# A two-layer decoder trunk: the fill of a head pair in the order keys, V, queries, little of it in the pair's last step, and more of the memory attentions' fill in their drain

## The chip, the cores and the metric

The kernel runs on one core of a Trainium2 chip. The metric is the device time of one execution in microseconds (us), lower is better. The engines are TensorE (PE; PEld is its weight load, which runs beside the matmuls), VectorE (DVE), ScalarE (ACT), GpSimd (POOL), and the queue of SyncE (SP), which issues the DMAs.

## The reference, cut to what matters

The input x is 1024 tokens by 1024 features, the memory 256 tokens. There are two layers, each x <- LayerNorm(alpha x + y W_out). In both, one part of y is a 4-head cross-attention into the memory, gated by silu. The other part is a pooling branch in layer 0 and, in layer 1, a causal attention of 16 heads of 64 with forget gates, whose keys and values come from one shared projection:

```python
def forgetting_attention(u, k, v, cum):
    ...
        logits = jnp.einsum('bqhd,bkhd->bhqk', qi, k,
                            preferred_element_type=jnp.float32) * scale
        logits = logits + (ci[..., :, None] - cum_k[:, :, None, :])
    ...
        logits = jnp.where(mask[None, None], logits, -jnp.inf)
        p = jax.nn.softmax(logits, axis=-1)
        return jnp.einsum('bhqk,bkhd->bqhd', p.astype(v.dtype), v)

def mixer_sublayer(x, mem, w_in, w_mem_kv, w_out, main_fn):
    h = x @ w_in
    ...
    y = jnp.concatenate([y_main * jax.nn.silu(g_main), y_mem * jax.nn.silu(g_mem)], axis=-1)
    return y @ w_out
```

All is float32.

## The kernel before, in words

**Products.** A float32 operand is kept as a high and a low part in a rounded float32 format, and a product is three matmuls (high·high, high·low, low·high). The unit of a projection is `slab` (L171 to L188): 128 output features by 1024 tokens, 48 matmuls of 128x512 with float32 accumulation in two PSUM banks of the three named `pj`. The weights come in two pieces, each loaded by SP into `raw` (three buffers) and split into high and low (`split_w`, L145 to L154; in the attention stage by POOL). The order is piece 0 for the token halves n = 0 and 1, 12 matmuls each, then piece 1 for n = 0 and 1. When a bank is complete its `evac` function is issued: after matmul 36 for the first 512 tokens, after matmul 48 for the others. `slab` is a generator: it yields after each matmul, so other code can be put between.

**Stages, in time.** Pool group 0 and the memory's keys and values for layer 0 (to about 110 us), memory attention 0 (to about 195), pool groups 1 to 3 (to about 340), the output projection with LayerNorm of layer 0 (to about 480), the memory's keys and values and memory attention 1 (about 535 to 625), the start units (first V, forget gates, the first pair's keys and queries, to about 684), the forgetting attention `fox` (684 to 1136), and the output projection of layer 1 (to the end).

**What sets the order.** PE's order is the order of the code, written out by hand within `manual_schedule` (L312, L771). The order on DVE, ACT, POOL and SP is set by the tile scheduler. `Fill` (L42 to L63) is a list of such generators; `pump(cols)` issues matmuls until `cols` columns (512 each) are due, so projections are spread as fill over the steps of an attention.

**`mem_attention`** (L259 to L325). After the memory queries, four gates' slabs (4 x 48 matmuls) are the fill of a loop of ten steps t. In steps 0 to 7 `probs(t)` makes the softmax of four heads for 128 tokens: logits on PE, maximum on DVE, Exp on ACT, the normalised probabilities in two half-precision parts on ACT and DVE (the latter is L294), and a transposing DMA. In the odd steps from 3 on, `values` makes O for 256 tokens and four heads; one PSUM bank `O` is read each time by DVE (L310). Steps 8 and 9 are the drain. Five calls of `pump` in each step issue a `part` of what is left (L314, L317, L321).

**`fox`** (L717 to L769). Sixteen heads, two to a pair, so eight pairs; eight steps to a head, from tile 7 (128 queries by 1024 keys) down to tile 0 (128 by 128). After head 15 come five steps without logits. A step is:
- `probs` (L631 to L657): POOL applies the causal mask to the row of forget gates (L640); PE makes the logits into a bank `L` (L169); DVE adds the gates and takes the extreme value (L647); ACT makes Exp into a bank `T` (L653).
- between logits and Exp, `halves` of the tile before (L659 to L672): DVE normalises (L664 to L667), ACT (L670) and DVE (L671) write two half-precision parts.
- 40% of the step's fill (`FRAC`), then `turn` (L676): a transposing DMA on SP's queue.
- for an even tile of five steps ago (`LAG`), `values` (L682 to L697): O on PE, read by ACT (L696) and DVE (L697); in the odd head also `pair_out` on POOL.
- 60% of the fill.

The fill of a pair p > 0 is what pair p + 1 needs, from `pair_units` (L604 to L610): the keys' slab (`k_evac`, L583 to L589, with two swaps of halves by DMA), the queries' slab, and V's slab for p + 1 >= 2. The queries' `q_evac` (L594 to L599) has for each half of 512 tokens and for each head of the pair one ACT copy (L596) and one DVE subtraction (L597), 64x512 each. V's bank is copied by ACT (L609) to `u`; `values_of` (L490) takes the maximum (L236), scales and splits it (L237 to L244) and turns it by two DMAs (L500). The V of pairs 0 and 1 was made in the start units (`first_vs`). Pairs 0, 2, 4 and 7 have gates' slabs added behind; pair 0's fill is the remainder of pair 1's units after the start units; pair 7 has the late gates.

What is left of the fill is divided over the steps left of the pair by `SHARE` (L39), all ones; pair 7's also over the five steps of the drain (L742, L743). At the end of an odd head the rest is issued (L768, L769). A pair's 144 matmuls are thus 9 in each of its 16 steps (12 in pairs 2 and 4).

Of the kernel before, what the change touches and what calls it, by code (L numbers as in the profile page):

```python
# [35 lines left out]
LAG = 5  # L36
APART = 6 * NH
PSCALE = 2.0 ** 15
SHARE = (1,1,1,1,1,1,1,1)  # L39


class Fill:  # L42
# [29 lines left out]
def trunk_kernel(ctx, tc, x, xT, memT, win, wk, wv0, wv, wmk, wmv, wout, poolw, pscale, lng, lnb, bforget, out):  # L72
# [186 lines left out]
    def mem_attention(l, XH, XL, kv, qtile, ytile, yd):  # L259

        kh, kl, v, undo = kv
        qs = []
        for h in range(MH):
            qh, ql = qtile(), qtile()
            run(slab(win[l, 8 + h], XH, XL, lambda cols, acc: hi_lo(qh[:, cols], ql[:, cols], acc)))
            qs.append((qh, ql))
        ys, gs = [ytile() for _ in range(MH)], [G() for _ in range(MH)]
        pt, fill = {}, Fill()
        for h in range(MH):
            fill.add(gate_units(win[l, 20 + h], gs[h], XH, XL), SLAB)  # L270

        def probs(i):

            p, two = sb([P, MH, NMEM], "P", 4), sb([P, 2, MH, NMEM], "P", 4, F16)
            m, ms, sm, r = tiny(MH), tiny(MH), tiny(MH), tiny(MH)
            for hp in range(2):
                lg = ps([P, 2, NMEM], "L", 2)
                for j in range(2):
                    h = 2 * hp + j
                    qh, ql = (t[:, i * P : (i + 1) * P] for t in qs[h])  # L280
                    mm3(lg[:, j, :], ((qh, kh[:, h, :]), (qh, kl[:, h, :]), (ql, kh[:, h, :])))
                pair = slice(2 * hp, 2 * hp + 2)
                nc.vector.tensor_reduce(m[:, pair], lg, AX.X, ALU.max, negate=True)
                nc.vector.tensor_scalar(ms[:, pair], m[:, pair], MSCALE, None, ALU.mult)
                for j in range(2):
                    h = 2 * hp + j
                    nc.scalar.activation(
                        p[:, h, :], lg[:, j, :], AF.Exp, bias=ms[:, h : h + 1], scale=MSCALE, accum_out=sm[:, h : h + 1],
                    )
            nc.vector.tensor_scalar(r, sm, 1.0 / PSCALE, None, ALU.mult)  # L290
            nc.vector.reciprocal(r, r)
            for h in range(MH):
                nc.scalar.activation(two[:, 0, h, :], p[:, h, :], AF.Copy, scale=r[:, h : h + 1])
                nc.vector.scalar_tensor_tensor(  # L294
                    two[:, 1, h, :], p[:, h, :], r[:, h : h + 1], two[:, 0, h, :], ALU.mult, ALU.subtract,
                )
            pt[i] = T([P, 2, MH, 2, P], F16)
            nc.sync.dma_start_transpose(
                pt[i].rearrange("p e h m q -> p (e h m) q"), two.rearrange("p e h t -> p (e h t)"),
            )  # L300

        def values(c, h):
            acc = ps([P, 2 * P], "O", 1)
            for j in range(2):
                t = pt[2 * c + j]
                mm3(acc[:, j * P : (j + 1) * P], [
                    (v[:, h, 2 * e + m, :], t[:, f, h, m, :])
                    for m in range(2) for e, f in ((0, 0), (0, 1), (1, 0))
                ])
            nc.vector.tensor_scalar(ys[h][:, c * 2 * P : (c + 1) * 2 * P], acc, undo[:, h : h + 1], None, ALU.mult)  # L310

        with tc.manual_schedule(engines={PE}):  # L312
            for t in range(ST + 2):
                part = fill.left / (5 * (ST + 2 - t))  # L314
                if t < ST:
                    probs(t)
                fill.pump(part if t <= ST else 3 * part)  # L317
                for h in range(MH):
                    if t >= 3 and t % 2 == 1:
                        values((t - 3) // 2, h)  # L320
                    fill.pump(part if t <= ST else part / 2)  # L321
            fill.pump(float("inf"))
        for h in range(MH):
            nc.vector.tensor_tensor(ys[h], ys[h], gs[h], ALU.mult)  # L324
            nc.sync.dma_start(yd[:, h, :], ys[h])  # L325
# [150 lines left out]
    with tc.tile_pool(name="in1", bufs=1) as in1:  # L476

        def xy():
            return sb([P, S], "B", 10, F32R, in1)
# [98 lines left out]
        def qk_units(p):  # L578

            halves = (slice(0, 64), slice(64, P)), (slice(64, P), slice(0, 64))  # L580
            ks, ws = ([xy() for _ in range(2)] for _ in range(2))

            def k_evac(cols, acc):  # L583
                for t, w, (own, other) in zip(ks, ws, halves):
                    nc.scalar.copy(t[own, cols], acc[own, :])
                    nc.vector.tensor_tensor(t[other, cols], acc[own, :], t[own, cols].bitcast(F32), ALU.subtract)
                    if cols.stop == S:
                        for to, of in ((own, other), (other, own)):
                            nc.sync.dma_start(w[to, :].bitcast(F32), t[of, :].bitcast(F32))  # L589

            yield from slab(wk[p], XH, XL, k_evac)
            qs = [xy() for _ in range(2)]

            def q_evac(cols, acc):  # L594
                for t, (own, other) in zip(qs, halves):
                    nc.scalar.activation(t[own, cols], acc[own, :], AF.Copy, scale=-0.125)  # L596
                    nc.vector.scalar_tensor_tensor(  # L597
                        t[other, cols], acc[own, :], -0.125, t[own, cols].bitcast(F32), ALU.mult, ALU.subtract,
                    )  # L599

            yield from slab(win[1, p], XH, XL, q_evac)
            pairs[p] = list(zip(qs, ks, ws))

        def pair_units(p):  # L604

            yield from qk_units(p)
            if p >= 2:
                u = MK([P, S], F32)
                yield from slab(wv[p - 2], XH, XL, lambda cols, acc: nc.scalar.copy(u[:, cols], acc))  # L609
            pairs[p].append(first_vs[p] if p < 2 else values_of(u))  # L610

        def start_units(own, following):

# [103 lines left out]
        def fox(following):  # L717
# [8 lines left out]
            for hd in range(HEADS + 1):  # L726
                pr, b = divmod(hd, 2)
                if hd < HEADS:
                    if b == 0:
                        o, sums = G(), sb([P, 4 * ST], "sums", 2, F32, small).rearrange("p (n b i) -> p n b i", n=2, b=2)  # L730
                        if 0 < pr < 7:
                            fill.add(pair_units(pr + 1), 3 * SLAB)
                        for ahead in {0: (0, 1), 2: (2,), 4: (4,), 7: (7,)}.get(pr, ()):
                            gate_ahead(ahead)
                        if pr == 0:
                            fill.add(following, SLAB)
                        for late in (3, 5, 6) if pr == 7 else ():
                            fill.add(late_gate(late), SLAB)
                    R, ahead_R = ahead_R, None
                for i in range(ST if hd < HEADS else LAG):  # L740
                    tile_of = ST - 1 - i
                    ahead = sum(SHARE[i:]) + (sum(SHARE) if b == 0 else 0) + (sum(SHARE[:LAG]) if pr == 7 else 0)  # L742
                    part = fill.left * SHARE[i] / (ahead if hd < HEADS else sum(SHARE[i:LAG]))  # L743
                    new, split = None, []

                    def behind():
                        if fresh[0]:
                            split.append(halves(*fresh[0]))
                            fresh[0] = None

                    if i == 2 and hd < HEADS - 1:
                        ahead_R = forget_rows(hd + 1)
                    if hd < HEADS:
                        new = (hd, tile_of, o)
                        fresh[0] = probs(hd, tile_of, R, sums, behind)
                    else:
                        behind()
                    fill.pump(part * FRAC[0])
                    for what in split:
                        turn(*what)  # L760
                    older = past[0]
                    if older and older[1] % 2 == 0:
                        values(older[0], older[1] // 2, older[2])
                        if older[0] % 2:
                            pair_out(older[0] // 2, older[1] // 2, older[2], gs.get(older[0] // 2))
                    fill.pump(part * (1 - FRAC[0]))
                    past = past[1:] + [new]
                if b and pr < 7 or hd == HEADS:  # L768
                    fill.pump(float("inf"))  # L769
# [71 lines left out]
```

## Time and profile before

| | |
|---|---|
| runs | 1290.47, 1286.43, 1284.64 us |
| median | 1286.43 us |
| the profiled execution | 1286.64 us |
| its span in the trace | 1284.6 us |
| mean granted TensorE clock | 0.993 |
| busy share of the span | PE 97%, PEld 81%, DVE 62%, ACT 45%, POOL 13% |
| matmuls with their line | 2928 of L181 (the slabs) 724.7 us; 384 logits 91.8 us; 1152 of O in `fox` 76.2 us |

A row of a timeline is: start, duration, engine, line, operation, output tile <- input tiles, shapes, count, and in brackets the idle time before it with what ended it. A row like `PE L L169 <- DVE s L647: 6.3, 10, 1.2` in the view of waits reads: PE at the tile L (line 169) waited for DVE's line 647, in all 6.3 us, 10 times, at most 1.2. Matmuls overlap: a matmul of 128x512 is shown with about 0.4 us, while the next one starts sooner.

### The profile page before, as it was taken

Reading aid. Unit: us, or ns where it says so; the run is one execution under the profiler, and the core shown is the slowest. Engines: PE = TensorE matmul, PEld = TensorE weight load, DVE = VectorE, ACT = ScalarE, POOL = GpSimd, SP = SyncE. Lnnn points to the kernel's source line nnn. Section 1 sums busy time; section 2 is a strip of 40 time slices with the busy share of each in tenths; the row PEclk is TensorE's granted clock in tenths of the full one; section 3 lists DMA queues with packets and bytes.
Section 4 is the critical chain, followed back from the end, with each engine's and each line's share of the span. In section 5 each row is a group of like instructions: output and inputs, shape, how many; then the busy total and the mean of one; then the engine's idle time right before and its main releaser. Section 6 shows DMA issues by size and latency. Waiting matters only on the chain. (4 is left out here: it accounts for less than half of the span.)

```text
span 1284.6 us, 19666 instructions
## 1 busy us (share of the span) xinstructions
PE 1250.4 (97%) x7018; PEld 1036.3 (81%) x7018; DVE 802.6 (62%) x1904; ACT 578.7 (45%) x1272; POOL 169.2 (13%) x267
## 2 busy tenths in 40 slices
PE   9999999999999999999999999999999999989997
PEld 6888878888778889887887788887888778867885
DVE  6452766356575457267455778777777888756444
ACT  5332642132431124265225667766766677643110
POOL 0000000000000000000003334333334233320000
PEclk9999999999999999999999999999999999989999
DMA  6351433213573226134516766968867786786330
GB/s 220 117 148 50 107 96 108 84 57 116 174 230 113 98 81 186 54 85 116 163 50 154 152 154 164 193 143 180 179 163 181 165 200 162 183 263 208 116 115 33
DMA packets 267410, 178.65 MB, mean 139 GB/s; under 512 B 212272, under 2 KB 225712, under 8 KB 267312
## 3 DMA queue, kind: packets, MB, share of 16 engines
q1 hardware_dynamic: 267312, 177.40, 51.3%
q8 instruction: 55, 0.90, 0.3%
q14 instruction: 43, 0.35, 0.1%
HBM read 94.97 MB, written 22.61 MB: 92 GB/s over the span
## 5 line engine op out<-in xcount | busy, mean ns | idle before, releaser
L181 PE MATMUL pj<-A,w 128*128 128x512 f32 x2928 | 724.7, 395 | 1.0 <-ACT A L142 1.0
L181 PEld LDWEIGHTS pj<-A,w 128*128 128x128 f32 x2928 | 537.5, 189 | 104.5 <-ACT A L142 2.4
L153 DVE TENSOR_TENSOR w<-raw,w 128x512 fp32r<-128x512 f32 x102 | 70.2, 689 | 112.6 <-ACT w L152 111.7
L653 ACT ACTIVATE T<-MK,s 128x512 f32<-128x512 f32 x192 | 110.8, 577 | 55.4 <-DVE s L647 41.3
L152 ACT CAST w<-raw 128x512 fp32r<-128x512 f32 x102 | 63.1, 620 | 156.5 <-PE pj L181 102.6
L671 DVE SCALAR_TENSOR_TENSOR P<-T,s,P 128x512 f16<-128x512 f32 x192 | 111.6, 614 | 31.6 <-ACT P L670 29.6
L670 ACT ACTIVATE P<-T,s 128x512 f16<-128x512 f32 x192 | 102.5, 575 | 46.3 <-ACT T L653 18.7
L169 PE MATMUL L<-B,B 128*128 128x512 f32 (+3 forms) x384 | 91.8, 343 | 8.5 <-DVE s L647 6.3
L169 PEld LDWEIGHTS L<-B,B 128*128 128x128 f32 x384 | 70.0, 188 | 30.0 <-DVE s L647 14.6
L559 POOL MEMSET G<- 128x128 f32 x1 | 0.2, 205 | 618.1 <-DVE V L324 618.1
L647 DVE CUSTOM_DVE_ANT_0 MK<-L,R 128x512 f32<-128x512 f32 (+3 forms) x128 | 73.0, 570 | 13.0 <-PE L L169 7.5
L169 PEld LDWEIGHTS <-V 128*128 128x128 f16 x1152 | 65.4, 99 | 18.9 <-issue 18.2
L169 PE MATMUL O<-T,V 128*128 128x128 f16 x1152 | 76.2, 221 | 1.3 <-DVE G L697 1.3
L142 ACT CAST T<-T 128x1024 fp32r<-128x1024 f32 x24 | 25.2, 1052 | 103.4 <-DMA T<-y1d 52.7
L153 POOL TENSOR_TENSOR w<-raw,w 128x512 fp32r<-128x512 f32 x54 | 69.7, 1290 | 4.1 <-PE pj L181 0.2
L143 DVE TENSOR_TENSOR T<-T,T 128x1024 fp32r<-128x1024 f32 x24 | 29.3, 1222 | 61.0 <-PE L L355 57.4
L640 POOL TENSOR_SCALAR_AFFINE_SELECT R<-R 128x128 f32<-128x128 f32 x128 | 40.6, 320 | 175.9 <-DVE s L647 100.2
L150 POOL TENSOR_SCALAR w<-raw 128x512 fp32r<-128x512 f32 x54 | 35.8, 663 | 143.6 <-PE pj L181 143.1
L355 PE MATMUL pj<-B,T 128*128 128x512 f32 x216 | 53.3, 395 | 1.0 <-DVE B L143 1.0
L355 PE MATMUL L<-B,T 128*128 128x512 f32 x216 | 51.9, 389 | 0.0
L213 PE MATMUL pj<-T,w 128*128 128x256 f32 x384 | 48.4, 285 | 1.3 <-ACT w L152 0.8
L355 PEld LDWEIGHTS pj<-B,T 128*128 128x128 f32 x216 | 41.1, 191 | 10.5 <-DVE B L143 1.8
(180 smaller groups left out, 1595.9 us busy)
## 6 DMA issues: line engine op xcount, KB each, us to landing
raw<-in_win_dram SPq DMA_DIRECT2D x96, 256.0 KB, 2.7
raw<-in_wout_dram SPq DMA_DIRECT2D x48, 256.0 KB, 3.2
B<-B SPq DMA_DIRECT2D x32, 256.0 KB, 4.1
R<-cumd SPq DMA_DIRECT2D x16, 512.0 KB, 4.4
y0d<-Y SPq DMA_DIRECT2D x12, 512.0 KB, 2.6
T<-y0d SPq DMA_DIRECT2D x12, 512.0 KB, 4.1
T<-y1d SPq DMA_DIRECT2D x12, 512.0 KB, 4.0
raw<-in_wmk_dram SPq DMA_DIRECT2D x16, 256.0 KB, 2.7
```

The lines of the kernel that those rows point to most:

```text
L150: nc.gpsimd.tensor_scalar(h, r, 1.0, 1.0, ALU.mult, ALU.mult)
L152: nc.scalar.copy(h, r)
L153: (nc.gpsimd if low[0] else nc.vector).tensor_tensor(l, r, h.bitcast(F32), ALU.subtract)
L169: nc.tensor.matmul(acc, a, b, start=i == 0, stop=i == len(terms) - 1)
L181: nc.tensor.matmul(accs[n], a[:, k, :], b[:, kt, n * NH : (n + 1) * NH], start=kt == 0 and i == 0, stop=kt == KT - 1 and i == 2,)
L213: nc.tensor.matmul(acc, w[:, k, :], m[pc][:, k, :], start=pc == 0 and k == 0 and i == 0, stop=pc == 1 and k == 3 and i == 2,)
L355: nc.tensor.matmul(accs[a][nh], y[:, k, a * P : (a + 1) * P], w, start=kt == 8 and i == 0, stop=kt == 7 and i == 2,)
L640: nc.gpsimd.affine_select(R[:, qs], R[:, qs], [[-1, P]], ALU.is_ge, -NEG, base=0, channel_multiplier=1)
L647: nc.vector.tensor_tensor_reduce(p[:, lo:up], lg, R[:, lo:up], 1.0, top, ALU.add, ALU.min, m[:, n : n + 1])
L653: nc.scalar.activation(e, p[:, lo:up], AF.Exp, bias=top, scale=-1.0, accum_out=sums[:, n, hd % 2, i : i + 1],)
L670: nc.scalar.activation(pair[:, lo:up], e, AF.Copy, scale=r)
L671: nc.vector.scalar_tensor_tensor(pair[:, L + lo : L + up], e, r, pair[:, lo:up], ALU.mult, ALU.subtract)
```

## The change

Three things. In `mem_attention`, the steps before the drain divide what is left as if two more steps were to come. In `fox`, the shares are all ones for the even head of a pair and 1, 1, 1, 1, 1, 1, 1, 0.25 for the odd one; the drain after head 15 and its part of pair 7's count stay five equal ones. In `pair_units`, V's slab with `values_of` is put between the keys' and the queries'; for that `qk_units` returns the two generators, and the queries' tiles are taken from their pool when the first of them is written.

```diff
-SHARE = (1,1,1,1,1,1,1,1)
+SHARES = (1,) * 8, (1,) * 7 + (0.25,)
...
             for t in range(ST + 2):
-                part = fill.left / (5 * (ST + 2 - t))
+                part = fill.left / (5 * (ST + 2 - t)) if t >= ST else fill.left / (5 * (ST + 4 - t))
...
-            yield from slab(wk[p], XH, XL, k_evac)
-            qs = [xy() for _ in range(2)]
+            qs = []
 
             def q_evac(cols, acc):
+                if not qs:
+                    qs.extend(xy() for _ in range(2))
+                    pairs[p] = list(zip(qs, ks, ws))
...
-            yield from slab(win[1, p], XH, XL, q_evac)
-            pairs[p] = list(zip(qs, ks, ws))
+            return slab(wk[p], XH, XL, k_evac), slab(win[1, p], XH, XL, q_evac)
 
         def pair_units(p):
 
-            yield from qk_units(p)
+            keys, queries = qk_units(p)
+            yield from keys
             if p >= 2:
                 u = MK([P, S], F32)
                 yield from slab(wv[p - 2], XH, XL, lambda cols, acc: nc.scalar.copy(u[:, cols], acc))
-            pairs[p].append(first_vs[p] if p < 2 else values_of(u))
+                v = values_of(u)
+            yield from queries
+            pairs[p].append(first_vs[p] if p < 2 else v)
...
-                    ahead = sum(SHARE[i:]) + (sum(SHARE) if b == 0 else 0) + (sum(SHARE[:LAG]) if pr == 7 else 0)
-                    part = fill.left * SHARE[i] / (ahead if hd < HEADS else sum(SHARE[i:LAG]))
+                    ahead = sum(SHARES[b][i:]) + (sum(SHARES[1]) if b == 0 else 0) + (LAG if pr == 7 else 0)
+                    part = fill.left * SHARES[b][i] / (ahead if hd < HEADS else LAG - i)
```

## The prediction

> **What bounds the kernel now.** I read the page's first part, the waits of TensorE in the attention stage, that stage's busy times, and then the timelines at the places where the change moves work.
>
> ```profile
> span 1284.6 us, 19666 instructions
> ## 1 busy us (share of the span) xinstructions
> PE 1250.4 (97%) x7018; PEld 1036.3 (81%) x7018; DVE 802.6 (62%) x1904; ACT 578.7 (45%) x1272; POOL 169.2 (13%) x267
> ```
>
> ```profile
> 684.00:1119.00 435.00, 426.49 (x2734) 348.85 (x2733) 340.04 (x992) 303.58 (x715) 153.86 (x249) 1.00 0.76 172
> ```
>
> ```profile
> PE L L169 <- DVE s L647: 6.3, 10, 1.2
> PE L L169 <- DVE B L597: 1.8, 1, 1.8
> ```
>
> TensorE (PE) is busy for 97% of the span. The second fence is the forgetting attention in the table of windows (start:end, length, then PE, PEld, DVE, ACT, POOL busy, clock, DMA share, GB/s): PE is busy 426.49 of 435.00 us. So the change can win back at most 8.5 us there, and each new hole in PE's row is paid in full. The third fence gives the holes by cause: 6.3 us in ten waits for the logits' reader (L647), and 1.8 us in a single wait for the copy of queries (L597). That single wait is at the one place where before already has a pair's queries filled last, between pairs 0 and 1 (first_vs gives V there):
>
> ```profile
> 731.30 0.34 PE L169 MATMUL L<-B,B 128*128 128x128 f32 x2
> 731.47 2.28 PE L181 MATMUL pj<-A,w 128*128 128x512 f32 x9
> 735.57 0.97 PE L169 MATMUL L<-B,B 128*128 128x512 f32 x3 [1.81 <-DVE B L597]
> ```
>
> ```profile
> 734.08 0.59 ACT L596 ACTIVATE B<-pj 64x512 fp32r<-64x512 f32 x1
> ```
>
> ```profile
> 734.82 0.69 DVE L597 SCALAR_TENSOR_TENSOR B<-pj,B 64x512 fp32r<-64x512 f32 x1
> ```
>
> The smallest tile's logits (call them L128) start at 731.30 and nine fill matmuls end at 733.75. The queries' last half must then pass ScalarE (734.08 + 0.59) and VectorE (734.82 + 0.69 = 735.51), since the next pair begins with tile 7, which reads query columns 896 to 1023. Handing over takes 0.15 and 0.06 us. From L128 to the next pair's first logits it is 735.57 - 731.30 = 4.27 us. The clock answers to such a hole:
>
> ```profile
> 176.80:180.20 3.40, 1.68 (x18) 1.25 (x15) 2.90 (x7) 1.68 (x5) 0.00 (x0) 1.00 0.30 82
> 180.20:183.60 3.40, 3.40 (x21) 2.86 (x19) 0.48 (x1) 0.00 (x0) 0.00 (x0) 1.00 0.68 154
> 733.20:736.60 3.40, 1.59 (x7) 0.99 (x6) 2.80 (x9) 2.39 (x6) 1.88 (x2) 1.00 0.60 158
> 736.60:740.00 3.40, 3.40 (x21) 2.68 (x20) 1.88 (x5) 1.41 (x3) 0.54 (x2) 0.50 0.98 228
> ```
>
> ```profile
> 1139.40:1146.20 6.80, 6.13 (x14) 4.84 (x15) 6.48 (x7) 2.86 (x5) 4.47 (x2) 0.50 0.79 256
> ```
>
> After the hole at 733.75 the granted clock is 0.50 for 3.4 us (fourth row). After an almost equal hole in the memory attention (first row) it stays at 1.00 (second row). A longer one, at the end of the stage, costs two such stretches (the last fence).
>
> **The change part by part.** The built order of the changed kernel shows it does what it says. In pairs 1, 3, 5 and 6 the keys end in the even head, V's slab follows, and the queries come last. The last step of each odd head has 2 fills instead of 9, and those 2 are the queries' last two matmuls, directly ahead of the next pair's first logits. The other steps get 9 to 10. In pairs 2 and 4 a gate's slab still comes last.
>
> A. The boundaries 1→2, 3→4, 5→6, 6→7. Before, at 1→2, there is no hole:
>
> ```profile
> 787.16 0.34 PE L169 MATMUL L<-B,B 128*128 128x128 f32 x2
> 787.33 2.28 PE L181 MATMUL pj<-A,w 128*128 128x512 f32 x9
> 789.45 0.84 PE L169 MATMUL L<-B,B 128*128 128x512 f32 x3
> ```
>
> ```profile
> 787.95 0.29 DVE L647 CUSTOM_DVE_ANT_0 MK<-L,R 128x128 f32<-128x128 f32 x1
> 788.17 0.08 DVE L647 DVE_READ_ACCUMULATOR2_ANT s<- 128x1 f32 x1
> 788.51 0.48 DVE L671 SCALAR_TENSOR_TENSOR P<-T,s,P 128x256 f16<-128x256 f32 x1 [0.26 <-ACT P L670]
> ```
>
> ```profile
> 788.01 0.47 ACT L670 ACTIVATE P<-T,s 128x256 f16<-128x256 f32 x1
> 788.38 0.36 ACT L653 ACTIVATE T<-MK,s 128x128 f32<-128x128 f32 x1
> 788.67 0.19 ACT L653 ACTIVATION_READ_ACCUMULATOR T<-MK,s 128x1 f32 x1
> ```
>
> L128 to the next logits: 789.45 - 787.16 = 2.29 us. In the changed order the queries' last copy stands on ACT behind this Exp, its read and the 256-wide L670, and on DVE behind L647 and the 256-wide L671. By hand: L128 at 787.16, Exp and read done at 788.86, L670 0.47, L596 0.59, L597 0.69, handovers 0.21, together 790.8 or 3.7 us. If one copy of the first half is still in the way as well, another 0.59 + 0.69 gives 5.0. I take 4.27, the row of the same event, which lies between. The distance grows by 1.98. The 7 fills that leave the step run in other steps, where PE has no room: by the fills of two rows (this one and the tail's, below) one takes (3.19 - 2.28) / 4 = 0.23, so 1.6. Each boundary costs 3.6, four cost +14.4 (12 to 17). Behind the waiting logits all of PE's queue stands, so DVE's next L647 and the Exp behind it start late by the same amount; I count that once.
>
> B. The boundary 0→1 has the chain already; its 7 fills move too, and the chain then starts from L128 instead of from the last fill. +1.3 (1.0 to 1.6).
>
> C. The clock. Two fills end about 0.7 us after they start (2.28 less seven times 0.23), 0.84 after L128, so each hole of A lasts 4.27 - 0.84 = 3.4 us, twice the one that was followed by 3.4 us at 0.50. Half speed for 3.4 us is 1.7 us of work lost, four times +6.8 (0 if none, 13.6 if each has two stretches as in the last fence of clocks). The Trainium skill, page "TensorE: Matmul & The Clock Gate", section "HAM oscillation — how this bites in real kernels", says that idle gaps have to be over about 3.4 us for the clock to fall back; the row at 733.20 has it fall after 1.81, so the measurement decides for a cost here. By the rule this term would be near 0 and the sum 1300.
>
> E. The heavy steps of the odd heads. There the queries' four L597 (4 × 0.69 = 2.8 us of DVE) go out and V's work comes in:
>
> ```profile
> L500 SPq DMA_TRANSPOSE V<-MK x16: 1241/1322/1873, 663.2 to 1077.2; - x16
> L609 ACT COPY MK<-pj x12: 562/586/588, 787.3 to 1070.4; 128x512 f32<-128x512 f32 x12
> L236 DVE TENSOR_REDUCE s<-MK x8: 1208/1220/1220, 658.2 to 1071.0; 128x1 f32<-128x1024 f32 x8
> L243 ACT ACTIVATE MK<-MK,s x8: 1137/1149/1152, 660.6 to 1073.1; 128x1024 f16<-128x1024 f32 x8
> L244 DVE SCALAR_TENSOR_TENSOR MK<-MK,s,MK x8: 1279/1282/1335, 661.9 to 1074.6; 128x1024 f16<-128x1024 f32 x8
> ```
>
> ```profile
> 776.26 0.68 DVE L597 SCALAR_TENSOR_TENSOR B<-pj,B 64x512 fp32r<-64x512 f32 x1
> 776.98 0.56 DVE L647 CUSTOM_DVE_ANT_0 MK<-L,R 128x384 f32<-128x384 f32 x1
> ```
>
> ```profile
> 777.60 0.73 PE L169 MATMUL L<-B,B 128*128 128x512 f32 x2 [0.55 <-DVE s L647]
> ```
>
> The last two fences show a stall of that kind: L597 ahead of L647, and PE late by 0.55. V brings 1.22 + 1.28 us and some small ones, so about as much, now in steps 0 to 3 of the odd head. I expect the stalls to move and not to go; one more fill in a step covers 0.23, four times: -1.0 (from -6.3, all waits on L647 gone, to +2.0, two more of the largest size). The two transposes of V stand on SP's queue 1.3 us each among those of the weights; a turned tile is read five steps later, so I cost them at nothing, and at up to 2 × 1.3 per pair if that lead were used up. V's weight loads move ahead of the queries' on SP with the same three buffers: nothing. POOL splits the same weights in another order: nothing.
>
> F. The memory attentions. Step 7 of each has a hole before:
>
> ```profile
> 176.86 1.17 PE L181 MATMUL pj<-A,w 128*128 128x512 f32 x4
> 179.76 0.83 PE L169 MATMUL O<-T,MK 128*128 128x128 f16 x12 [1.73 <-DVE Y L310]
> ```
>
> ```profile
> 177.64 1.67 DVE L294 SCALAR_TENSOR_TENSOR P<-P,s,P 128x256 f16<-128x256 f32 x4
> 179.22 0.48 DVE L310 TENSOR_SCALAR Y<-O,undo 128x256 f32<-128x256 f32 x1
> ```
>
> ```profile
> 606.59 0.83 PE L169 MATMUL O<-T,MK 128*128 128x128 f16 x12 [1.72 <-DVE V L310]
> ```
>
> PE waits for the O bank behind four L294 in one go (1.67 us). In the changed order this L310 stands ahead of them, so the wait goes. Late next are the four L294, by 0.5 (the L310), with fewer fills to cover in the steps before the drain (about 16 instead of 19). -1.73 - 1.72 + 2 × 0.5 = -2.4 (-3.5 to +1.0).
>
> G. The last step of head 15 loses six fills too:
>
> ```profile
> 1119.50 3.19 PE L181 MATMUL pj<-A,w 128*128 128x512 f32 x13
> 1122.76 0.23 PE L169 MATMUL O<-T,V 128*128 128x128 f16 x1
> ```
>
> Its 13 fills cover the landing of the tile turned for O; with 7 O waits. 6 × 0.23 = +1.4 uncovered at most; I take +1.2 (0 to 1.4). The fills themselves go to other steps as before. The boundaries 2→3 and 4→5, with a gate last, I cost at nothing: L647 reaches the small tile before the fills end, as at 787.95.
>
> The profiled run took 1286.64 us, 2.0 more than its span and 0.2 more than the median of 1286.43. Sum: 1286.6 + 14.4 + 1.3 + 6.8 - 1.0 - 2.4 + 1.2 = **1306.9, say 1307 us**.
>
> **The rivals.** 1. *The wait comes, the clock stays.* For it speaks the hole of 1.73 us at 177, after which the clock stayed at 1.00; against it, that A's holes are twice as long. 1307 - 6.8 = 1300.
>
> 2. *It is worse than the row.* A copy of the first half stands ahead as well (5.0 instead of 4.27: 4 × 0.73 = 2.9), the longer hole has two stretches of half clock as at 1139 (+6.8), and V's work adds stalls (+2.0 instead of -1.0). 1307 + 12.7 = 1319. DVE at 340 of 435 us busy in the stage speaks for it, the hand-made chain of 3.7 against.
>
> 3. *The copies are through in time; not slower.* The mechanism: with few fills around it, the last step leaves ACT and DVE empty, and the copy runs ahead of the older work. It decides at 1.0 us after L128: if L596 starts by then, 0.59 + 0.69 end at 2.3 us, the distance of before. Then A costs only its fills (6.4), C nothing, the boundary 0→1 loses its own extra 1.98 and its half clock (-3.7 beside B's 1.3), and with the light last step the waits on L647 go (-6.3): 1286.6 + 6.4 + 1.3 - 3.7 - 6.3 - 2.4 + 1.2 = 1283. Against it: Exp of L128 alone starts 1.2 us after L128 (788.38), and the built order puts it and an L670 ahead of L596.
>
> **How the numbers follow.** The forecast 0.45, rival 1 0.22, rival 2 0.18, rival 3 0.10; 0.05 for rival 3 with F's full -3.5 and E's other gains, about 1279. About 0.5% (6.4 us) is what a measurement of this kernel can tell from no change: below 1280 is faster, to 1293 the same. Faster: the last case and a part of rival 3, 0.07. Same: the rest of rival 3 and a little of rival 1's lower end (A at 12, E at -3), 0.10. Slower 0.83. The range 1291 to 1319 holds the forecast and rival 1 with A from 12 to 17 and half of rival 2, and leaves out rival 3 and the longest chains.
>
> **What would show it.** In the waits of TensorE: five waits of L on L597 of about 3.4 us each, at the starts of heads 2, 4, 8, 12 and 14, instead of one of 1.8; that is A, and it falls if L to L over these places stays near 2.3. In the windows behind them: 3.4 us at 0.50; C falls at 1.00. The waits on L647 stay between 3 and 8 us (E). Those on L310 (1.73, 1.72) are gone (F), and O's first matmul in head 15's last step has a wait of about a microsecond (G). The prediction is wrong if the queries' last L596 starts within 1.0 us of L128.

## The result, and the profile after

The changed kernel takes 1306.65 us (median of 6 runs, 1300.91 to 1308.38) against 1286.61 us before (6 runs); the ratio is 1.0139, 95% interval 1.012 to 1.0158, some 18 us slower (15 to 20). The forecast was 1307.

The page of the changed kernel, first part:

```profile
span 1304.3 us, 19672 instructions
## 1 busy us (share of the span) xinstructions
PE 1259.8 (97%) x7018; PEld 1042.8 (80%) x7018; DVE 801.6 (61%) x1904; ACT 581.3 (45%) x1272; POOL 163.7 (13%) x267
```

The span grew by 19.7 us. DVE, ACT and POOL do the same work as before; PE's busy time grew by 9.4 us with the same 7018 matmuls, which is a slower clock, and the rest is idle time of PE. The waits of TensorE from 684 to 1160 us (what waited, for what: us in total, times, longest):

```profile
PE L L169 <- DVE B L599: 15.3, 5, 3.4
PE pj L355 <- ACT T L142: 3.5, 1, 3.5
PE L L169 <- DVE s L651: 3.5, 9, 0.5
PE O L169 <- DVE G L701: 0.8, 1, 0.8
```

The logits' wait for the queries' copy (L597 before, L599 now) is 15.3 us in five waits instead of 1.8 in one. That for the logits' reader (L647, now L651) is 3.5 instead of 6.3. Here is the boundary 1→2, first PE's timeline, then ACT's and DVE's:

```profile
787.86 0.33 PE L169 MATMUL L<-B,B 128*128 128x128 f32 x2
788.03 0.68 PE L181 MATMUL pj<-A,w 128*128 128x512 f32 x2
792.07 1.38 PE L169 MATMUL L<-B,B 128*128 128x512 f32 x4 [3.36 <-DVE B L599]
```

```profile
789.93 0.37 ACT L657 ACTIVATE T<-MK,s 128x128 f32<-128x128 f32 x1 [0.71 <-DVE s L651]
790.23 0.19 ACT L657 ACTIVATION_READ_ACCUMULATOR T<-MK,s 128x1 f32 x1
790.33 0.45 ACT L674 ACTIVATE P<-T,s 128x256 f16<-128x256 f32 x1
790.68 0.58 ACT L598 ACTIVATE B<-pj 64x512 fp32r<-64x512 f32 x1
```

```profile
788.89 0.49 DVE L701 SCALAR_TENSOR_TENSOR G<-O,unscale,G 64x256 f32<-64x256 f32 x1
789.41 0.15 DVE L670 TENSOR_SCALAR s<-sums 128x1 f32<-128x1 f32 x1
789.59 0.29 DVE L651 CUSTOM_DVE_ANT_0 MK<-L,R 128x128 f32<-128x128 f32 x1
...
790.81 0.48 DVE L675 SCALAR_TENSOR_TENSOR P<-T,s,P 128x256 f16<-128x256 f32 x1
791.33 0.69 DVE L599 SCALAR_TENSOR_TENSOR B<-pj,B 64x512 fp32r<-64x512 f32 x1
```

Read it as a chain. PE finishes its two fills by 788.7. DVE reaches the small tile (L651) at 789.59, since the reader of O (L701) stands ahead. Then come the Exp at 789.93, the 256-wide L674, and only then the queries' last copy (L598 at 790.68, L599 to 792.02). The next pair's logits start at 792.07, 4.21 us after L128.

The windows below have their edges where the clock changes. The columns are start:end, length, busy us of PE, PEld, DVE, ACT and POOL, granted clock, DMA share, GB/s:

```profile
734.84:738.25 3.41, 1.52 (x7) 1.27 (x8) 2.18 (x9) 1.93 (x5) 2.02 (x3) 1.00 0.65 160
789.46:792.87 3.41, 0.80 (x3) 0.68 (x4) 2.34 (x10) 2.18 (x6) 2.57 (x3) 1.00 0.76 192
792.87:796.28 3.41, 3.41 (x13) 2.42 (x12) 2.12 (x5) 1.18 (x3) 0.54 (x2) 0.51 0.89 231
905.51:908.92 3.41, 1.22 (x7) 0.70 (x5) 2.75 (x11) 2.64 (x9) 1.88 (x2) 1.00 0.85 202
908.92:912.34 3.42, 2.29 (x5) 1.82 (x6) 2.40 (x6) 1.17 (x3) 0.00 (x0) 0.51 0.87 226
912.34:915.75 3.41, 3.41 (x18) 2.58 (x17) 1.53 (x5) 1.60 (x4) 0.59 (x2) 0.50 0.51 124
```

After the hole at 788.7 the clock is half for one window, after that at 906.7 for two; the holes at 1025.8 and 1084.3 are like the second. After the hole at the boundary 0→1 (734.8 to 736.7) it stays at 1.00.

### The profile page after: what moved, and what is told of

It reads as the page before. It is cut to its first block, busy times and chain, and to the rows that moved or that the text cites. A ratio compares the mean times of both kernels' runs of the same rounds, so it can differ in the third digit from the quotient of the medians.

```text
span 1304.3 us, 19672 instructions
## 1 busy us (share of the span) xinstructions
PE 1259.8 (97%) x7018; PEld 1042.8 (80%) x7018; DVE 801.6 (61%) x1904; ACT 581.3 (45%) x1272; POOL 163.7 (13%) x267
## 5 line engine op out<-in xcount | busy, mean ns | idle before, releaser
L674 ACT ACTIVATE P<-T,s 128x512 f16<-128x512 f32 x192 | 103.3, 576 | 38.1 <-ACT T L657 16.5
L169 PE MATMUL L<-B,B 128*128 128x512 f32 (+3 forms) x384 | 94.3, 352 | 18.9 <-DVE B L599 15.3
L651 DVE CUSTOM_DVE_ANT_0 MK<-L,R 128x512 f32<-128x512 f32 (+3 forms) x128 | 72.8, 569 | 15.8 <-PE L L169 12.2
L644 POOL TENSOR_SCALAR_AFFINE_SELECT R<-R 128x128 f32<-128x128 f32 x128 | 37.7, 298 | 185.7 <-DVE s L651 78.8
```

What stands on the lines that cost most here:

```text
L169: nc.tensor.matmul(acc, a, b, start=i == 0, stop=i == len(terms) - 1)
L644: nc.gpsimd.affine_select(R[:, qs], R[:, qs], [[-1, P]], ALU.is_ge, -NEG, base=0, channel_multiplier=1)
L651: nc.vector.tensor_tensor_reduce(p[:, lo:up], lg, R[:, lo:up], 1.0, top, ALU.add, ALU.min, m[:, n : n + 1])
L674: nc.scalar.activation(pair[:, lo:up], e, AF.Copy, scale=r)
```

## The experiments

"Theory" is: the next pair's logits wait for the queries' last copy, and TensorE's clock falls after the hole. All ratios are to the kernel before, with a 95% interval.

**The queries' halves exchanged.** On the changed kernel:

```diff
-    def slab(pieces_dram, XH, XL, evac, banks=("pj", 3)):
+    def slab(pieces_dram, XH, XL, evac, banks=("pj", 3), ns=(0, 1)):
...
-            for n in range(2):
+            for n in ns:
...
-slab(win[1, p], XH, XL, q_evac)
+slab(win[1, p], XH, XL, q_evac, ns=(1, 0))
```

> The changed kernel, with one difference: the queries' slab computes the second 512 tokens before the first 512 (in both weight pieces). Same fills, same shares, same order keys, V, queries; the last bank now holds the queries of tiles 0 to 3, which the next pair reads only in its fifth step. Theory (the next pair's first logits wait for the queries' last copy, and the clock falls in that hole): the five waits on L599 go (15.3 us idle in the changed kernel's trace) and with them the half clock behind four of them (about 10.5): 1306.7 - 25.8 = 1281 us, and no stretch at 0.50 between 690 and 1130 us. Rival (the light last step itself is the cost, whatever stands last in it: DVE reaches the small tile 1.7 us late and all after it): L to L stays near 4.2 us with another wait named, 1300 us or more.

Measured: 1286.46 us, ratio 1.0006 (0.9994 to 1.0018). No stretch at half clock is left in the attention stage, and its waits of TensorE begin

```profile
PE L L169 <- DVE s L651: 9.0, 14, 1.6
```

with none on L599. One exchange of two loop steps takes 20 us back. But for smaller terms of either sign (2.7 us more on the reader than before, 2.2 us of the memory attentions, shown below, and 3.5 us less at the boundary 0→1, its hole and its half clock), the wait on the copy, with the clock behind it, is the loss. The rival has a small part of the truth. At the boundary 1→2 the timeline of PE now reads

```profile
785.65 0.33 PE L169 MATMUL L<-B,B 128*128 128x128 f32 x2
785.83 0.68 PE L181 MATMUL pj<-A,w 128*128 128x512 f32 x2
786.34 0.62 PE L169 MATMUL L<-B,B 128*128 128x512 f32 x2
787.71 0.50 PE L169 MATMUL L<-B,B 128*128 128x512 f32 x1 [0.74 <-DVE s L651]
```

The next tile's third logits matmul needs the bank of the small tile, and DVE reads that late. With this and the longer waits in the odd heads the waits on L651 are 9.0 us, not 3.5, which is why the time is not the 1281 expected.

**The order alone.** The changed kernel with `SHARES = (1,) * 8, (1,) * 8` and the old `part` in `mem_attention`.

> The changed kernel with all shares one and the memory attentions as before: only the order keys, V, queries. Theory: the copy is released by the chain of about 4.2 us behind L128, so with 9 fills in the step the hole is 1.8 instead of 3.4 us at each of five boundaries; a fill that stays in the step costs nothing there. Four new boundaries cost 1.9 each (+7.6), with half clock behind none to all of them (0 to 6.8), less up to 4 for the waits on the logits' reader: 1288 to 1301, 1294 likeliest. Rival (it is the order alone that costs, and the light step adds nothing): 1306, like the changed kernel.

Measured: 1299.49 us, ratio 1.0114 (1.009 to 1.0138). Waits of TensorE in the stage:

```profile
PE L L169 <- DVE s L651: 9.7, 13, 1.9
PE L L169 <- DVE B L599: 9.0, 5, 1.8
```

The five holes are 1.8 us each, as the theory had it, and the clock fell behind one of them. But the waits on the reader are 9.7 us, not fewer than the 6.3 of before: V's work on DVE holds it up as much as the queries' copies did, and more. V's maximum (L236, 1.22 us) and the small steps behind it stand directly ahead of the reader at the four longest of these waits (1.09, 1.92, 0.94 and 1.95 us). So the time lies in the expected range, but 5.5 us above the likeliest 1294; the rival's 1306 did not come either. The order alone makes 12.9 of the 20 us.

**The shares alone.** The kernel before with the new `SHARES` and their two lines in `fox`.

> The kernel before with the new shares alone: V still last, so the last step's two fills belong to V, which nothing in the next head's first step reads. Theory: no wait on the queries' copy but at the boundary 0 to 1 (there it shortens from 4.27 to 2.8 us), the moved fills run where PE has some waits to fill: 1280 to 1288, 1285 likeliest. Rival (the light step starves TensorE by itself): four holes of over 2 us at the other boundaries too, waiting for L647 or a bank, 1300 us.

Measured: 1292.11 us, ratio 1.0039 (1.0024 to 1.0054). Both were wrong. The boundaries cost next to nothing, as the theory said, but in heads 3 and 11 the queries' copies now fall between the logits' readers in another way. PE's timeline in head 3 and its windows:

```profile
768.10 0.73 PE L169 MATMUL L<-B,B 128*128 128x512 f32 x2 [1.03 <-DVE s L647]
770.14 0.80 PE L169 MATMUL L<-B,B 128*128 128x256 f32 x2 [1.31 <-DVE s L647]
```

```profile
766.16:769.57 3.41, 1.64 (x7) 0.71 (x5) 3.28 (x7) 1.29 (x3) 0.77 (x2) 1.00 0.89 279
769.57:772.98 3.41, 2.84 (x14) 2.22 (x15) 2.68 (x9) 2.82 (x7) 1.87 (x4) 0.50 0.69 157
772.98:776.40 3.42, 3.42 (x15) 2.84 (x13) 2.44 (x4) 2.61 (x7) 0.06 (x1) 0.50 0.62 123
```

Two holes of about a microsecond close together make a window that is 48% busy, and two windows at half clock follow; the same happens in head 11, from 998.2 us. In head 7 two such holes (0.88 and 1.31 us) fall into two windows, and the clock stays at 1.00.

**Matmuls of zeros in the hole.** On the changed kernel, after the last fill of the odd heads of pairs 1, 3, 5 and 6 (`warm2` is a tile of zeros):

```diff
+                if b and pr in (1, 3, 5, 6):
+                    keep = ps([P, NH], "O", 1)
+                    for _ in range(13):
+                        nc.tensor.matmul(keep, warm2[:, :P], warm2, start=True, stop=True)
```

> The changed kernel with 13 matmuls of zeros (128x512, half-width type, into the O bank, read by nobody) issued behind the last fill at the boundaries 1-2, 3-4, 5-6 and 6-7, some 3.0 of the 3.4 us of each hole. They do no work of the reference. Theory: the waits on L599 stay (as the matmuls of zeros and 0.3 to 0.4 us of idle time together), the clock stays at 1.00 behind all four, and the time falls by what half clock costs, about 10.5: 1296 us. Rival (half clock has another cause than the hole, or costs nothing because other engines bound the steps behind it): 1306 us, with stretches at 0.50 still there or without.

Measured: 1298.03 us, ratio 1.0086 (1.0072 to 1.01); 8.6 us under the changed kernel. PE's timeline at the boundary 1→2, and the 6.8 us behind it:

```profile
791.43 0.33 PE L171 MATMUL L<-B,B 128*128 128x128 f32 x2
791.60 0.68 PE L183 MATMUL pj<-A,w 128*128 128x512 f32 x2
792.97 2.97 PE L779 MATMUL O<-warm 128*128 128x512 bf16 x12 [0.69 <-DVE G L703]
795.61 1.25 PE L171 MATMUL L<-B,B 128*128 128x512 f32 x4
```

```profile
795.60:802.40 6.80, 6.80 (x48) 5.73 (x47) 4.32 (x11) 3.92 (x8) 1.35 (x4) 1.00 0.61 147
```

From L128 to the next logits it is still 4.18 us, so the wait is unchanged, and the clock is whole behind all four. Useless work makes the kernel faster. The 8.6 us is the price of the half clock, a little too low: in the profiled execution the boundary 0→1, which got no zeros, had one stretch of it, which the changed kernel's had not. From the smallest tile of head 3 to that of head 14, which holds all four boundaries and not that one, the traces take 326.3 us without and 317.2 us with the zeros, 9.1 us less.

**The memory attentions.** First the kernel before with the new `part` alone, then the changed kernel with the old one.

> The kernel before with the memory attentions' new division alone. As forecast in the prediction (the 1.73 and 1.72 us waits go, 0.5 is late next in each): 2.4 us less, 1284.2. As the changed kernel's trace has it (the one large wait of each layer comes back as four smaller ones at earlier O's, 2.1 us a layer in all, as before, and fewer fills cover the steps before the drain): 0 to 2 us more, 1287.5.

> The changed kernel with the memory attentions as before: order and shares alone. By the forecast the memory part gained 2.4, so 1309; by the trace it gained nothing or lost up to 2, so 1305 to 1306.

Measured: alone 1288.79 us, ratio 1.0024 (1.0013 to 1.0035); left out 1301.28, ratio 1.0121 (1.0101 to 1.0142). So the memory part costs 1.7 to 4.5 us where it stands alone; beside the rest, where the two intervals overlap, the times don't tell the difference. The traces do. From the first logits of memory attention 1 to the first matmul behind its fill (L532), the eight kernels with the old division all take 80.6 us and the four with the new one 82.5 to 82.6. In layer 0, from the first logits to the start of the last O, it is 70.4 to 70.6 against 70.7 to 70.8. So the part costs about 2.2 us. PE's waits in the kernel with it alone, and two of its steps in layer 1:

```profile
PE O L169 <- DVE Y L310: 2.1, 4, 1.0
PE O L169 <- DVE V L310: 2.0, 4, 1.0
```

```profile
551.89 1.60 PE L169 MATMUL L<-MK,B 128*128 128x256 f32 x12
553.32 4.04 PE L181 MATMUL pj<-A,w 128*128 128x512 f32 x17
557.53 1.89 PE L169 MATMUL L<-MK,B 128*128 128x256 f32 x12 [0.16 <-ACT P L287]
```

The wait of 1.73 us went, and four shorter ones came at earlier O's, in all 2.1 us a layer as before. And with 17 fills between them where before had 20, the second step's logits wait for the Exp of the first: 1.89 instead of 1.60. The next two steps' logits are like it in the changed kernel (1.88 each); together that is about half of layer 1's 2.0 us, and the rest is not placed.

**The kernel before, its queries' halves exchanged**, and **the order alone, so exchanged**.

> The kernel before with the queries' slab computing its second 512 tokens first, nothing else. Theory (only the boundary 0 to 1 has the wait in before, 1.81 us, with half clock for 3.4 us behind it): the wait and the stretch at 0.50 near 737 us go, 1.8 + 1.7: 1283.1. Rival (the wait is inferred wrongly; the next logits wait for the reader of the small tile or a bank): the hole stays with another releaser, 1286.6.

> Order keys, V, queries with the queries' second 512 tokens first, all shares one, memory attentions as before. Theory (with 9 fills in the last step and no wait on the copy nothing is left of the boundaries' cost; the order by itself only moves the waits on the logits' reader): order alone less its five holes (9.0 us) and one stretch of half clock (1.7): 1288.8; if the stalls in the odd heads are not longer than in before, 1283. Rival (the order costs by V's work on VectorE, not by the holes): 1295 or more.

Measured: the first 1284.77 us, ratio 0.9998 (0.9984 to 1.0013). In its trace the hole and the half clock at 0→1 are gone, as expected: L128 starts at 731.63 and the next logits at 733.92, 2.29 us later. But the waits on L647 are 7.6 us in 14 instead of 6.3 in ten, one of them 1.8 us long in head 7 with half clock behind it. No gain in time can be told. The second 1291.66 us, ratio 1.004 (1.0026 to 1.0054): no holes at the boundaries, but

```profile
PE L L169 <- DVE s L651: 11.4, 14, 2.8
```

is the longest sum of such waits of all runs. The order without the light step and without the hole costs by V's work on DVE, as the rival said, though less than it said: V's maximum stands ahead of the reader at the four longest of these waits (1.22, 1.72, 1.11 and 2.78 us).

**A version that beats both.** The queries' halves exchanged, the changed order and shares, the old memory attentions; and the same with 0.6 for the last step.

> The changed kernel's fill order and shares, with the queries' second 512 tokens first and the memory attentions as before. Theory (the parts add: q_second_half_first measured 1286.5, and the memory part alone costs 2 to 3 on the kernel before): 1283.5 us, about 0.2% under the kernel before. Rival (the memory part's cost was met only in that run, or comes back at the start of the attention stage): 1286.5.

> The same with 0.6 instead of 0.25 for the odd head's last step, some 5 or 6 fills instead of 2. Theory (with 2 fills the next pair's third logits wait 1.05 us at four boundaries for the reader of the small tile, L651, which comes 1.7 us late; three or four more fills, 0.7 to 0.9 us, cover most of it, and are missing in the other steps only where TensorE is the bound anyway): the four waits fall to 0.2 to 0.4 us and the time by 2 to 3: 1281 us. Rival (the wait only moves to the odd heads' heavy steps, which lose fill): as q2_no_mem, within 1 us.

Measured: 1283.24 us, ratio 0.9961 (0.9944 to 0.9978), the one kernel here whose interval lies under 1, by 3 to 7 us; and 1289.22 us, ratio 1.002 (1.0006 to 1.0035). The waits of TensorE on the reader, in the first and in the second:

```profile
PE L L169 <- DVE s L651: 7.3, 12, 1.6
```

```profile
PE L L169 <- DVE s L651: 8.9, 18, 1.8
```

The theory for 0.6 fell. The waits at the four boundaries (0.74 to 0.78 us in the first kernel, not the 1.05 that was expected) do go. But the fills that go back to the last step are missing in the odd heads' heavy steps, where DVE is late: the rival's mechanism, at more than the rival's price, since the time is 6 us more. PE's rows show only 1.6 us of it; the weight loads (PEld) ahead of the logits wait 21.4 instead of 15.9 us for L651 between 684 and 1119 us, and 2.1 us for L599, which is the size of it. The light last step is worth something, once nothing waits for its fill: 1283.24 with it, 1291.66 with all shares one.

## Why the prediction was right, step by step

The forecast of 1307 met the measured 1306.65, and its largest step, A, is right in mechanism and nearly in size. The other terms were off by up to 5 us each and cancelled; that the sum came within 1 us of the time is luck.

| step | forecast | measured | from |
|---|---|---|---|
| A four boundaries | +14.4 | +13.4 | the four holes: 15.3 us on L599 less the 1.95 of B |
| B boundary 0→1 | +1.3 | -1.6 | a hole of 1.95 instead of 1.81 us, and no half clock (-1.7) |
| C clock | +6.8 | +9.1 | the zeros, by the traces; half the time from each next logits to the end of its half clock gives 1.7 + 2.85 + 3.0 + 2.8 = 10.4 |
| E odd heads | -1.0 | -2.8 | 6.3 to 3.5 us on the reader |
| F memory attentions | -2.4 | +2.2 | 80.6 to 82.6 us in layer 1, 70.5 to 70.7 in layer 0; by the time of the part alone 1.7 to 4.5 |
| G tail | +1.2 | -0.5 | 0.8 instead of 1.3 us on L701 |

They add to 19.8, and the span grew by 19.7. So close an agreement is partly chance: already up to the first logits of memory attention 0, where the code is the same, the two traces differ by 0.5 us (123.2 and 122.7).

A. The distance from L128 to the next logits was taken from the row of the one boundary that had the wait (4.27) and came out within 0.1: 4.21, 4.17, 4.21 and 4.19 us. The forecast added to its growth 1.6 us for the fills that run elsewhere, an estimate, and had 3.6 us a boundary; the holes, which show both at once, are 3.33 to 3.36. The chain by hand gave 3.7 because it let L651 start 0.8 us after L128; it started 1.7 after.

B. Wrong in sign. The forecast let the distance shrink by only 0.3 us (1.6 of moved fills less 1.3). It shrank by 1.5, to 2.81, because DVE reaches the small tile 0.7 us after L128 there and not 1.7 as at the boundary 1→2, and the clock stayed at 1.00 behind the hole:

```profile
733.92 0.33 PE L169 MATMUL L<-B,B 128*128 128x128 f32 x2
734.10 0.68 PE L181 MATMUL pj<-A,w 128*128 128x512 f32 x2
736.73 1.20 PE L169 MATMUL L<-B,B 128*128 128x512 f32 x4 [1.95 <-DVE B L599]
```

```profile
734.66 0.28 DVE L651 CUSTOM_DVE_ANT_0 MK<-L,R 128x128 f32<-128x128 f32 x1
```

C. Right that the half clock comes, too small: it was sized at one window behind each hole, and three of the four holes had two, which the range had as its upper end. Rival 1 (the clock stays) is ruled out for these holes, and rival 2 came true in that one point. The zeros show that the loss is the clock's and not another engine's. The rule of idle gaps over about 3.4 us in the Trainium skill ("TensorE: Matmul & The Clock Gate", "HAM oscillation — how this bites in real kernels") does not hold here: the clock fell behind gaps of 3.3 us, of 1.8 (before, at 733.75), and of 1.03 and 1.31 close together. The forecast's own holes of 3.4 us stood at that rule's border, so the 1300 that it drew from the rule did not follow from it.

E. The stalls did lessen, but not by the change's own doing. Where the holes are removed and the order and shares kept, the waits on the reader are 9.0 us: the holes gave DVE the time to catch up. The step's own reason (V's work for the queries' copies, about equal) is what the order alone shows, 9.7 us; it expected too little of it.

F. The step that failed most: 2.2 us more where 2.4 less were forecast. It followed the one wait that would go and took L294 for what is late next; late were the earlier O's and the logits, which had lost fills in every step before the drain.

G. Wrong: O in head 15's last step did not wait at all. The turned tile had landed after 7 fills:

```profile
1140.68 1.83 PE L181 MATMUL pj<-A,w 128*128 128x512 f32 x7
1142.35 1.40 PE L169 MATMUL O<-T,V 128*128 128x128 f16 x22
```

Rival 3 (the copies are through in time) is ruled out by the first fences: L598 started 2.8 us after L128, not within 1.0.

Two slips in the prediction's working change nothing here: rival 2 adds to 1319.7 us and not to 1319, and rival 1's lower end by its own terms (A at 12, E at -3) is about 1296, above the 1293 up to which it was counted as the same.

## What to carry to other kernels

Before fill work is put last in a stage, ask who reads its output first: here half of the queries' output was needed at once and the other half only four steps later, and computing the needed half first was worth 20 us. Where TensorE is the bound, price a hole at its length and the slower clock behind it (the fills that left it are in that length already); taking fills from a step uncovers what they covered. When several small terms are summed, a right total does not show that each was right; the parts run alone do.

## What the runs showed of the hardware

The clock changes on a fixed grid of 3.413 us. In the changed kernel it falls at 792.87, 908.92, 1028.39 and 1086.41 us: 34, 69 and 86 times 3.413 us from the first, within 0.1 us. That agrees with the free-running window of 3413 ns in the Trainium skill ("TensorE: Matmul & The Clock Gate", "What's actually happening").

Which way it changes goes with how busy TensorE was in the window that ended. In the windows of the attentions, it fell after busy shares of 23%, 24%, 36% and 37% (changed kernel), 47% (before, at 733.2) and 48% (shares alone), and it stayed after 45% (first row of the windows above) and 49% (before, at 176.8); so the border is near half there, and these shares, with modelled ends, don't give it more sharply. It came back after windows that were 100% (792.87), 93% (shares alone, 1145.0) and 84% busy (memory part alone, 1145.5), and not after 67% (908.92) or 83% (769.57).

The busy share of the trace does not settle it everywhere. Among the start units, a window that is 64% busy (changed kernel, 669.99 to 673.40; 63% before, 668.34 to 671.75) is followed by half clock, and in the kernel with the memory part alone a window that is wholly busy (674.48 to 677.89) does not bring the clock back. All three hold the small float32 matmuls of the forget gates (L565), which the attentions don't have; no run here shows whether they are the reason.

So the same hole costs nothing, one window or two, by where it lies on the grid. The changed kernel and the one without the memory part have the same distances at the boundaries 0→1 (2.81 us) and 1→2 (4.2 us); behind them the clock is half for no window and one in the first, and for one and two in the second. Executions of the changed kernel spread from 1300.91 us at a mean clock of 0.991 to 1308.38 at 0.985.
